# A two-layer trunk (gMLP mixer, retention, two dense MLPs): residual by tokens throughout, and four more blocks of products by seven

## The chip, the cores and the metric

The kernel runs on one core of a Trainium2 chip. A core has a matrix engine (TensorE: PE, with its weight loads PEld) and four others: VectorE (DVE), ScalarE (ACT), GpSimd (POOL) and SyncE (SP), which here only starts DMA transfers. DMA transfers are started from queues of SP, ACT and POOL and are carried out by 16 DMA engines. Matrix products add up in PSUM, in eight banks of 128 partitions x 512 float32. The metric is the device time of one execution, in us.

## The reference, cut to what matters

512 tokens of 1024 features, float32, go through two layers. Layer 0 mixes tokens by a gated MLP in chunks of 128, layer 1 by retention with four heads; each is followed by a dense MLP with a squared ReLU.

```python
def squared_relu_mlp(h, w1, w2):
    a = jax.nn.relu(h @ w1)
    return (a * a) @ w2
...
    proj = xn @ w_in                       # 1024 -> q 1024, k 1024, v 2048, g 2048
    q, k, v, g = jnp.split(proj, ...)
    q, k = rotary(q, cos, sin), rotary(k, cos, sin)
    # per head: scores of q and k with decay, causal, times v
    o = rmsnorm(o, head_norm_g.reshape(H, dv)).reshape(B, S, H * dv)
    o = (o * jax.nn.silu(g.astype(f32))).astype(xn.dtype)
    return o @ w_out
...
    for i in range(DEPTH):
        h = rmsnorm(x, norm_mix_g[i])
        x = x + mixer_i(h)                 # gMLP (w_in 1024x4096, w_out 2048x1024) or retention
        h = rmsnorm(x, norm_ffn_g[i])
        x = x + squared_relu_mlp(h, mlp_w1[i], mlp_w2[i])   # 1024x4096, 4096x1024
    return rmsnorm(x, final_norm_g)
```

## The kernel before

**Products.** Every float32 operand is split into a high part hi and a low part lo (fp32r), and `mm3` computes a product by three matmuls: hi hi, hi lo, lo hi. A matmul has 128 partitions of weights and 512 columns. Weights stream through the chip in raw tiles of 1 MB (one DMA on SP's queue, L166), each of two pieces: ACT casts a piece to its high half (`wH`, L234), DVE subtracts it for the low half (`wL`, L241). A piece feeds 24 matmuls, or twelve where it is half of a product by seven.

**Order.** `step` appends a piece and the function that uses it to a list, which is then run through: the function emits the matmuls, then `refill` the cast of the third piece ahead and the low half of the second ahead (LOOK = 3), then come its hooks (`behind`), and its evacuation. Each engine works through its own instructions in the order in which they were emitted. So what is emitted first on DVE also runs first, whoever waits.

**Products by seven.** `seven` computes a block of four 512x512 products of weights with activations by seven products (Strassen's scheme as changed by Winograd), numbered s = 0 to 6 in the order of a plan. Weight sums are made by accumulating DMAs on POOL's queue (`add_up`, L207): first the sum `t1`, then two more sums in the same tile once its pieces have been split, and one separate sum; so four accumulating DMAs for each `seven`. Activation sums are made by `form(s)`, on DVE and ACT: two sums (`sa`), two casts, two low parts (`sp`). Products gather in banks `a`, `b`, `c` (two PSUM tiles each: `smva0`, `smva1`), and DVE adds a finished one to its output (L529).

**Tiles and layers.** The residual `xT` stands by features (features on partitions). Its norm is summed over squares (ACT, POOL) and spread over partitions by matmuls with ones (`wide_stats`, `spread`); up products are evacuated by DVE with ReLU and the norm's factor (L953), then squared by ACT (L954). In layer 0's dense MLP three of four blocks are made by seven into `tok`, and the fourth by plain products (`dn`, `down_last`), where `tok` is transposed back on PE (L1023) and added to `xT`. After retention `to_tokens` (L1282) transposes `xT` the other way. In retention the values of heads 0 and 1 are made by seven, those of heads 2 and 3 plainly (`v_unit`), and all gates plainly by features (`g_unit`). q and k are rotated by DVE's four products with two tables, and POOL's two additions (L1084, L1085). `av` multiplies scores and values by features, with 512, 384, 256 and 128 columns, and the head's norm is again a sum over partitions.

**PSUM.** Six banks go by the name `acc`, two by `mis` (transposes, sums over partitions, scores, av).

## Time and profile before

| What | us |
|---|---|
| time, median of 3 runs | 1354.7 (1354.36 to 1355.17) |
| span of the profiled execution | 1353.1 |
| PE busy | 1342.5 |
| DVE busy | 868.0 |
| ACT busy | 581.0 |
| POOL busy | 190.3 |

The page gives for the profiled execution its span, from the first instruction to the last; the runs' times contain that and what lies around it, 1.6 us by the median. In a row of busy times, x is the number of instructions; in a row of a group the last numbers are the mean of one, or the least, median and greatest duration in ns. In the chain of waits and in the timeline a row begins with the start and the duration in us; a record of a matmul reaches into the next one. A raw tile is named with the array that it was loaded from, and the numbers of buffers are left out.

### The profile page before, as it was taken

What the parts mean: (1) busy time and instruction counts of PE and PEld (TensorE: products, weight loads), DVE (VectorE), ACT (ScalarE), POOL (GpSimd) and SP (SyncE); (2) the same over time, 40 slices, a digit from 0 to 9 for tenths busy, and PEclk for the clock granted to TensorE, in tenths of its full rate; (3) what the DMA queues carried; (4) which work ended last, traced back from release to release, by engine and by line L of the source; (5) the groups of instructions that cost most, each with busy time, mean ns of one, the idle gap of its engine ahead of it and who ended that gap; (6) DMA issues with size and microseconds to landing.
All of it is one profiled execution on the core that took longest, in us unless ns stands there. A gap on an engine that the chain in (4) does not pass through costs nothing.

```text
span 1353.1 us, 15298 instructions
## 1 busy us (share of the span) xinstructions
PE 1342.5 (99%) x6106; PEld 1117.2 (83%) x6106; DVE 868.0 (64%) x1101; ACT 581.0 (43%) x827; POOL 190.3 (14%) x145
## 2 busy tenths in 40 slices
PE   9999999999999999999999999999999999999997
PEld 7888888888888888888888888888888888888886
DVE  7754456665656656678946456557494675665697
ACT  5655443235544434524533343224333543443464
POOL 4100121130100000012201101111221000100003
PEclk9999999999999999999999999999999999999999
DMA  8662221245674747515712122221126375686763
GB/s 304 169 166 81 90 94 63 93 151 152 149 203 127 215 129 182 167 61 191 172 63 93 63 90 91 85 93 64 63 94 201 106 182 140 169 202 172 198 171 94
DMA packets 124439, 182.43 MB, mean 135 GB/s; under 512 B 3200, under 2 KB 68304, under 8 KB 124368
## 3 DMA queue, kind: packets, MB, share of 16 engines
q1 hardware_dynamic: 105040, 143.17, 31.2%
q0 software_dynamic: 19008, 37.75, 16.2%
q8 instruction: 48, 0.79, 0.2%
q10 hardware_dynamic: 320, 0.53, 0.1%
q14 instruction: 23, 0.19, 0.0%
HBM read 179.35 MB, written 2.10 MB: 134 GB/s over the span
## 4 chain that ended last, share of the span: by engine, by line
PE 97%; DVE 2%; ACT 1%; POOL 0%; issue 0%; ACTq 0%; POOLq 0%; DVEq 0%
PE up L281 24%; PE qk L281 6%; PE u L281 6%; PE o L281 6%; PE g L281 6%; PE ro L281 6%; PE dn L281 2%; PE vv L281 2%; PE av L281 2%; PE v L852 2%; PE smva L281 2%; PE smwa L281 2%; PE v L281 2%; PE sm12a L281 2%; PE sm11a L281 2%; PE sm10a L281 2%
## 5 line engine op out<-in xcount | busy, mean ns | idle before, releaser
L241 DVE TENSOR_TENSOR wL<-raw,wH 128x1024 fp32r<-128x1024 f32 x235 | 305.0, 1301 | 43.8 <-ACT wH L234 15.6
L234 ACT CAST wH<-raw 128x1024 fp32r<-128x1024 f32 x235 | 245.3, 1045 | 63.5 <-ACT wH L234 8.9
L281 PE MATMUL up<-hH,wH 128*128 128x512 f32 x480 | 187.2, 390 | 0.2 <-ACT xtok L1283 0.2
L281 PE MATMUL up<-hH,wL 128*128 128x512 f32 x480 | 186.8, 389 | 0.0
L281 PE MATMUL up<-hL,wH 128*128 128x512 f32 x480 | 186.8, 389 | 0.0
L953 DVE SCALAR_TENSOR_TENSOR r<-up,wide 128x512 f32<-128x512 f32 x54 | 37.4, 692 | 153.6 <-PE up L281 146.2
L954 ACT ACTIVATE aF<-r 128x512 f32<-128x512 f32 x54 | 34.2, 633 | 222.6 <-DVE r L953 222.6
L281 PEld LDWEIGHTS up<-hH,wH 128*128 128x128 f32 x480 | 90.1, 188 | 18.9 <-ACT xtok L1283 0.5
L281 PEld LDWEIGHTS up<-hH,wL 128*128 128x128 f32 x480 | 90.1, 188 | 18.9
L281 PEld LDWEIGHTS up<-hL,wH 128*128 128x128 f32 x480 | 90.1, 188 | 18.7
L207 POOL DMA_DIRECT2D raw<-in_mlp_w_dram x25 | 33.1, 1381 | 437.9 <-DVE wL L241 193.1
L310 POOL TENSOR_TENSOR ssq<-ssq,sq 128x512 f32<-128x512 f32 x28 | 44.1, 1577 | 117.0 <-ACT sq L309 116.7
L241 DVE TENSOR_TENSOR wL<-more,wH 128x1024 fp32r<-128x1024 f32 x42 | 51.0, 1217 | 4.5 <-issue 3.0
L234 ACT CAST wH<-more 128x1024 fp32r<-128x1024 f32 x42 | 44.0, 1047 | 15.9 <-ACT wH L234 6.0
L281 PE MATMUL o<-yH,wH 128*128 128x512 f32 x128 | 50.8, 396 | 0.0
L281 PE MATMUL g<-hH,wH 128*128 128x512 f32 x128 | 50.5, 394 | 0.0
L281 PE MATMUL u<-hH,wH 128*128 128x512 f32 x128 | 50.2, 393 | 0.0
L281 PE MATMUL qk<-hH,wH 128*128 128x512 f32 x128 | 50.0, 391 | 0.0
L281 PE MATMUL ro<-ryH,wH 128*128 128x512 f32 x128 | 49.9, 390 | 0.0
L281 PE MATMUL u<-hH,wL 128*128 128x512 f32 x128 | 49.9, 390 | 0.0
L281 PE MATMUL ro<-ryH,wL 128*128 128x512 f32 x128 | 49.9, 390 | 0.0
L281 PE MATMUL g<-hH,wL 128*128 128x512 f32 x128 | 49.9, 390 | 0.0
(450 smaller groups left out, 3050.1 us busy)
## 6 DMA issues: line engine op xcount, KB each, us to landing
raw<-in_mlp_w_dram SPq DMA_DIRECT2D x50, 1024.0 KB, 5.1
raw<-in_mlp_w_dram POOLq DMA_DIRECT2D x25, 1024.0 KB, 8.8
raw<-in_b_w_in_dram SPq DMA_DIRECT2D x22, 1024.0 KB, 5.0
more<-in_mlp_w_dram SPq DMA_DIRECT2D x21, 1024.0 KB, 5.3
raw<-in_a_w_in_dram SPq DMA_DIRECT2D x10, 1024.0 KB, 5.3
raw<-in_a_w_out_dram SPq DMA_DIRECT2D x8, 1024.0 KB, 4.9
raw<-in_b_w_out_dram SPq DMA_DIRECT2D x8, 1024.0 KB, 4.8
morew<-in_a_w_in_dram SPq DMA_DIRECT2D x5, 1024.0 KB, 8.5
```

What stands on the lines that cost most here:

```text
L207: nc.gpsimd.dma_start(out=r.tile, in_=src, accum_op=ALU.add)
L234: nc.scalar.copy(out=p.hi, in_=p.src)
L241: nc.vector.tensor_sub(out=p.lo, in0=p.src, in1=f32(p.hi))
L281: nc.tensor.matmul(ps, lhsT=a, rhs=b, start=start and i == 0, stop=stop and i == 2, skip_group_check=resumed)
L310: nc.gpsimd.tensor_tensor(out=state["ssq"], in0=state["ssq"], in1=sq, op=ALU.add)
L852: nc.tensor.matmul(accs0[n], lhsT=h[kk][:, n * P : (n + 1) * P], rhs=w, start=kk == 0 and j == 0, stop=kk == 7 and j == 2)
L953: nc.vector.scalar_tensor_tensor(out=r, in0=ps, scalar=0.0, in1=rbc, op0=ALU.max, op1=ALU.mult)
L954: nc.scalar.activation(a, r, AF.Square)
```

## The change

- **Residual by tokens.** `tok`, two tiles with tokens on partitions, holds the residual from x to the end. Inputs of products (`hH`, `hL`) are its transposes: `turn` on PE, then ACT (high part, with the norm's gain) and DVE (low part). The row's norm is a sum that ACT gathers along a row (`tsq`), and its factor is applied later: to q and k through the two tables, to values and gates as a row's scale, in the dense MLP as the squared factor `r2s` when a product is added to `tok` (a ReLU commutes with a positive factor). Up products are evacuated by ACT alone: ReLU and Square. x is loaded again in layer 0's mixer, since its tiles are used in between. Sums of the input (`hF`) are made by adding the parts.
- **Dense.** Layer 0's fourth block is made by seven as layer 1's is (`dense_end`); `down_last`, `to_tokens` and the sums over partitions are gone.
- **Retention.** All values and all gates are made by seven: `v` and `w` (values of heads 0, 1 and 2, 3), `g` and `j` (gates). The four sums of the input that V forms are stored in DRAM (`keep_sums`, SP's queue) and fetched for W and J (`fetched`, POOL's queue). `av` has tokens on partitions, and its result, multiplied by the gate and the head's norm, is transposed (`turned`). The rotation's additions are DVE's, and its tables lie in `wide`, where the norm's factors were broadcast.
- **Order.** A script, played by `play`, lists retention's pieces (q also for k, o and s for the output) with the work behind each in brackets.

```diff
-    xT2 = [big([P, 4, T], F32, f"xT{b}") for b in range(2)]
-    xT = [xT2[k // 4][:, k % 4, :] for k in range(KD)]
-    hH, hL = [None] * KD, [None] * KD
+    tok = [big([P, NT, 512], F32, f"tok{c}") for c in range(2)]
...
+    def turn(ps, k, ns=range(NT)):
+        for n in ns:
+            nc.tensor.transpose(ps[:, n * P : (n + 1) * P], tok[k // 4][:, n, (k % 4) * P : (k % 4 + 1) * P], ident)
+
+    def chunk(k, ps, gcol):
+
+        fresh_h(k, gcol)
         g = gT[:, gcol + k : gcol + k + 1]
-        nc.vector.tensor_scalar_mul(hH[k], xT[k], g)
-        nc.vector.scalar_tensor_tensor(out=hL[k], in0=xT[k], scalar=g, in1=f32(hH[k]), op0=ALU.mult, op1=ALU.subtract)
-
-    def squares(k, gcol):
-        if k == 0:
-            state["ssq"] = tmp(f"ssq{gcol}", "ssq", 1)
-            nc.scalar.activation(state["ssq"], xT[k], AF.Square)
-        else:
-            sq = tmp(f"sq{gcol}_{k}", "sq")
-            nc.scalar.activation(sq, xT[k], AF.Square)
-            nc.gpsimd.tensor_tensor(out=state["ssq"], in0=state["ssq"], in1=sq, op=ALU.add)
+        nc.scalar.activation(hH[k], ps, AF.Copy, scale=g)
+        nc.vector.scalar_tensor_tensor(out=hL[k], in0=ps, scalar=g, in1=f32(hH[k]), op0=ALU.mult, op1=ALU.subtract)
+
+    def turned_chunk(k, gcol, bank=mis):
+        ps = bank(f"ht{k}")
+        turn(ps, k)
+        chunk(k, ps, gcol)
+
+    def add_parts(b):
+        whole[b] = big([P, 4, T], F32, f"hF{4 * b}")
+        for i in range(4):
+            nc.vector.tensor_add(out=whole[b][:, i, :], in0=f32(hH[4 * b + i]), in1=f32(hL[4 * b + i]))
+
+    def tsq(n, c):
+        nc.scalar.activation(tmp(f"tsq{n}{c}", "sq"), tok[c][:, n, :], AF.Square, accum_out=ssf[:, n, c : c + 1])
...
+    def root(dst, power):
+
+        a = work.tile([P, NT], F32, tag="ms", name="ms", bufs=2)
+        nc.vector.tensor_tensor(out=a, in0=ssf[:, :, 0], in1=ssf[:, :, 1], op=ALU.add)
+        nc.vector.tensor_scalar(out=a, in0=a, scalar1=1.0 / D, scalar2=EPS, op0=ALU.mult, op1=ALU.add)
+        nc.gpsimd.tensor_tensor(out=dst, in0=a, in1=power[:, 0:NT], op=ALU.pow)
...
+    def norm(name):
+
+        root(r4, mhalf)
+        yield
+        yield from spread(r4, rbc, name)
+
+    def norm_squares():
+
+        root(r2s[:, 0, :], mone)
+        nc.vector.tensor_scalar(out=r2s[:, 1, :], in0=r2s[:, 0, :], scalar1=-1.0, scalar2=0.0, op0=ALU.mult, op1=ALU.add)
...
+        def add_to(m, n, t, op, bank):
+
+            m, n = 2 * m + t, 1 - n if swap else n
+            v, sign = dst[n][:, m, :], op == ALU.subtract
+            if (m // 2, n) in fresh:
+                nc.scalar.activation(v, bank, AF.Copy, scale=-1.0 if sign else 1.0)
+            elif scaled:
+                nc.vector.scalar_tensor_tensor(out=v, in0=bank, scalar=r2s[:, int(sign), m : m + 1], in1=v, op0=ALU.mult, op1=ALU.add)
+            else:
+                nc.vector.tensor_tensor(out=v, in0=v, in1=bank, op=op)
...
+    def out_half(pl, ys, c, name, hooks={}, after=None, end=None):
+
+        accs, last = {}, 2 * len(pl) - 1
+
+        def mms(p, i, n):
+            for k in range(2):
+                kk = 2 * i + k
+                mm3(accs[n], *ys(kk, n), p.hi[:, k, :], p.lo[:, k, :], kk == 0, kk == last)
+
+        def add(n):
+            v = tok[c][:, n, :]
+            nc.vector.tensor_tensor(out=v, in0=v, in1=accs[n], op=ALU.add)
...
-            if ("rbc", l) in state:
-                r = zt(f"r{i}")
-                nc.vector.scalar_tensor_tensor(out=r, in0=ps, scalar=0.0, in1=rbc, op0=ALU.max, op1=ALU.mult)
-                nc.scalar.activation(a, r, AF.Square)
-                return
             nc.scalar.activation(a, ps, AF.Relu)
-            while ("rbc", l) not in state:
-                yield
-            nc.vector.tensor_mul(a, a, rbc)
             nc.scalar.activation(a, a, AF.Square)
-            yield
+            return iter(())
...
-    def down_last(gcol, ahead):
-
-        pl = pieces_f(mlp_w2[0], (3072, 4096), (0, D))
-        ev = evac_x(gcol)
-
-        def back(i):
-            ps = mis(f"yt{i}")
-            for n in range(NT):
-                nc.tensor.transpose(ps[:, n * P : (n + 1) * P], tok[i // 4][:, n, (i % 4) * P : (i % 4 + 1) * P], ident)
-            nc.vector.tensor_add(xT[i], xT[i], ps)
...
+    def dense_end(l, plan3, ahead, hooked, after3, last, more, middle=None):
+
+        pl = pieces_f(mlp_w1[l], (0, D), (3072, 4096))
+        hooks2, hooks3 = {}, {}
+        _, form2, prod2 = seven(mlp_w2[l], 2048, 0, side_a(4, f"{l}2"), tok, f"{l}2", (0, 1, 2, 3, 5, 4, 6), hooks2, scaled=True)
+        t3, form3, prod3 = seven(mlp_w2[l], 3072, 0, side_a(6, f"{l}3"), tok, f"{l}3", plan3, hooks3, after3, last, True, True, middle=middle)
...
+    def keep_sums(s):
+
+        stored[s] = dram.tile([P, 2, 4, T // 2], F32, name=f"sums{s}")
+        nc.sync.dma_start(out=stored[s], in_=f32(made["v", s]))
+
+    def fetched(s):
+        if s in (0, 2, 6):
+            return direct_h(s)
+        sp = big([P, 2, 4, T // 2], F32R, f"spx{s}")
+        nc.gpsimd.dma_start(out=sp, in_=stored[s])
+        return side_split(sp)
+
+    def twofold(c, dst, side, name, plan, swap=False):
+        return seven(bw, 0, c, side, dst, name, plan, swap=swap, new=True, auto=False)
+
+    PLAN_V = (0, 2, 1, 3, 4, 5, 6)
+    PLAN_G = (1, 4, 0, 3, 5, 2, 6)
+    sides = [kept(side_h("v")), kept(fetched)]
+    tV, form_v, prodV = zip(*[twofold(VW + 1024 * i, vF[i], sides[i], "vw"[i], (PLAN_V, PLAN_G)[i]) for i in range(2)])
+    tG, form_g, prodG = zip(*[twofold(GWT + 1024 * i, gF[i], sides[i], "gj"[i], PLAN_G, True) for i in range(2)])
...
-        nc.gpsimd.tensor_tensor(out=m[0], in0=m[0], in1=m[1], op=ALU.subtract)
-        nc.gpsimd.tensor_tensor(out=m[2], in0=m[2], in1=m[3], op=ALU.add)
+        nc.vector.tensor_sub(out=m[0], in0=m[0], in1=m[1])
+        nc.vector.tensor_add(out=m[2], in0=m[2], in1=m[3])
...
+    def av(h, n):
+
         vhi, vlo = vv[h]
         ph, pl = pp[h]
-        ps = mis(f"av{h}{c}")
-        cs = slice(c * P, (c + 1) * P)
-        for j in range(NT):
-            s = slice(POFF[j], POFF[j] + T - j * P)
-            mm3(ps[:, j * P :], vhi[:, j, cs], vlo[:, j, cs], ph[:, s], pl[:, s], j == 0, j == NT - 1)
+        assert {(x, h, j) for x in "pv" for j in range(n + 1)} | {("g", h, n)} <= ready, (h, n)
+        ps = mis(f"av{h}{n}")
+        for j in range(n + 1):
+            s = slice(POFF[j] + (n - j) * P, POFF[j] + (n - j + 1) * P)
+            mm3(ps, ph[:, s], pl[:, s], vhi[:, j, :], vlo[:, j, :], j == 0, j == n)
 
         def gen():
-            o = oo[h][:, c, :]
-            if c == 0:
-                state["ssqh"] = tmp(f"ssqh{h}", "ssq", 1)
-                nc.scalar.activation(state["ssqh"], ps, AF.Square)
+            y, ss, ms, r = gates(h)[:, n, :], ssh[:, h, n : n + 1], msh[:, h, n : n + 1], rh[:, h, n : n + 1]
+            nc.vector.tensor_tensor(out=y, in0=ps, in1=y, op=ALU.mult)
+            nc.scalar.activation(tmp(f"sqh{h}{n}", "sq"), ps, AF.Square, accum_out=ss)
+            yield
+            nc.vector.tensor_scalar(out=ms, in0=ss, scalar1=1.0 / DV, scalar2=EPS, op0=ALU.mult, op1=ALU.add)
+            rsqrt(r, ms, 1)
+            nc.scalar.activation(y, y, AF.Copy, scale=r)
+            ready.add(("y", h, n))
...
+        for n in range(NT):
+            nc.tensor.transpose(ps[:, n * P : (n + 1) * P], gates(h)[:, n, c * P : (c + 1) * P], ident)
+        g = gT[:, HG + 4 * h + c : HG + 4 * h + c + 1]
+        hi, lo = rH[h][:, c, :], rL[h][:, c, :]
+        nc.scalar.activation(hi, ps, AF.Copy, scale=g)
+        nc.vector.scalar_tensor_tensor(out=lo, in0=ps, scalar=g, in1=f32(hi), op0=ALU.mult, op1=ALU.subtract)
...
+    play("""
+        Q(w1,w0,R) v v v v(f1,k1) v(R,N) v(f3) q q v(f4) v v(f5,k4) v v(k5) v v(k3) v +G g g g(sc00,sc01)
+        g(sc02,sc03,vs00) g(vs01) g q g(vs02,vs03) g q g g g(si001) g(si02) q(si03,av03) q(av00,av02) g
+        q(sc10,sc11,si10) g(av01,sc12) q(si12,si13,sc13,vs10123) q(yt00,si11,yt01) q(yt02,av101,F3) o(yt03,av123)
+        o(yt10123) o(F4) +w o w o o w(F5) w o o w w w w w(F1) w w +j j w j w w(sc20) j w j(sc21,sc22) j(vs20) j(sc23)
+        q(vs22,vs23) j j(vs21) j q j(si21,si20,av21) q(si23,si22,av22,av20) q(av23) j(sc30,sc32) j(sc31)
+        j(yt20123,vs3012) -(vs33,si301) j(sc33) s(si323,av30123) s(yt30123) s s s(sq0123,ht0) s(ht2,ht3) s(ht1)
+    """, v=prodV[0], g=prodG[0], w=prodV[1], j=prodG[1], o=out_pair(0), s=out_pair(1, half_end(FFN + 8)),
+        Q=qs[:1], q=qs[1:])
```

On DVE before the change, where values of heads 0 and 1 are made by seven, from the third sum's operations (`sav`, `spv3`) on; `vF` is the output of values, `m01` the rotation of k of head 0 (L1080 to L1083):

```order
L618 SCALAR_TENSOR_TENSOR sav_4573<-xT0_86,gT_76,sav_4573 128x256 x4
L646 SCALAR_TENSOR_TENSOR spv3_4796<-sav_4573,spv3_4796 128x512 x2
L241 TENSOR_TENSOR wL146_4791<-raw67_4105,wH146_4790 128x1024
L529 TENSOR_TENSOR vF0_4545<-vF0_4545,smvb0_4772 128x512
L529 TENSOR_TENSOR vF0_4545<-vF0_4545,smvb1_4773 128x512
L241 TENSOR_TENSOR wL147_4818<-raw67_4105,wH147_4817 128x1024
L1080 TENSOR_TENSOR m010_4853<-qk02_4741,tab_4547 128x512
L1081 TENSOR_TENSOR m013_4856<-qk02_4741,tab_4547 128x512
L1082 TENSOR_TENSOR m011_4854<-qk03_4823,tab_4547 128x512
L1083 TENSOR_TENSOR m012_4855<-qk03_4823,tab_4547 128x512
L241 TENSOR_TENSOR wL148_4849<-raw74_4684,wH148_4848 128x1024
L618 SCALAR_TENSOR_TENSOR sav_4573<-xT1_87,gT_76,sav_4573 128x256 x4
```

Between two low halves stands one form, one pair of additions or one rotation's products. After the change, the same place starts with the first form, behind piece 147:

```order
L249 TENSOR_TENSOR wL149_4615<-raw71_4249,wH149_4614 128x1024
L593 TENSOR_TENSOR sav_4638<-hF0_4552,hF4_4547 128x512 x2
L616 TENSOR_TENSOR spv1_4637<-sav_4638,spv1_4637 128x512 x2
L503 TENSOR_TENSOR vF00_4597<-vF00_4597,smvb0_4600 128x512
L503 TENSOR_TENSOR vF00_4597<-vF00_4597,smvb1_4601 128x512
L249 TENSOR_TENSOR wL150_4631<-raw75_4545,wH150_4630 128x1024
L350 TENSOR_TENSOR sp_mix1_1_4668<-r4_80,sp_mix1_0_4667 128x4
L365 TENSOR_TENSOR dg0_mix1_4671<-ident_74,sp_mix1_0_4667 128x512
L365 TENSOR_TENSOR dg1_mix1_4673<-ident_74,sp_mix1_1_4668 128x512
L1243 TENSOR_TENSOR wide_79<-trg1_4466,wide_79 128x512
L1244 TENSOR_TENSOR wide_79<-trg0_4465,wide_79 128x512
L1138 TENSOR_TENSOR m000_4695<-qk0a_4473,wide_79 128x512
```

The additions of `smvb` stand behind the form; then come the norm's diagonals (`dg`, for the broadcast `wide`), the two tables (into `wide`) and the rotation of q, all before low half 151. The rotation's other two products and its two additions, low half 151 and the low parts of q (`qkL`), form 3, low halves 152 and 153, and a second rotation with its additions follow, then these:

```order
L249 TENSOR_TENSOR wL154_4781<-raw77_4635,wH154_4780 128x1024
L599 TENSOR_TENSOR sav_4638<-sav_4638,hF4_4547 128x512 x2
L616 TENSOR_TENSOR spv4_4818<-sav_4638,spv4_4818 128x512 x2
L249 TENSOR_TENSOR wL155_4815<-raw77_4635,wH155_4814 128x1024
L249 TENSOR_TENSOR wL156_4838<-raw78_4709,wH156_4837 128x1024
L602 TENSOR_TENSOR sav_4638<-hF0_4552 128x512 x2
L616 TENSOR_TENSOR spv5_4861<-sav_4638,spv5_4861 128x512 x2
L249 TENSOR_TENSOR wL157_4858<-raw78_4709,wH157_4857 128x1024
L503 TENSOR_TENSOR vF01_4723<-vF01_4723,smvc0_4649 128x512
L503 TENSOR_TENSOR vF01_4723<-vF01_4723,smvc1_4650 128x512
L249 TENSOR_TENSOR wL158_4883<-raw71_4249,wH158_4882 128x1024
L249 TENSOR_TENSOR wL159_4903<-raw71_4249,wH159_4902 128x1024
```

Forms 4 and 5 come, with one low half or two between, ahead of the additions of `smvc`, which come ahead of low halves 158 and 159.

On POOL before, the sums for values by seven (`raw67`, three times in one tile) stood between the rotation's additions:

```order
L207 DMA raw67_4105<-in_b_w_in_dram 128x4x512
L1084 TENSOR_TENSOR m000_4725<-m000_4725,m001_4726 128x512
L1085 TENSOR_TENSOR m002_4727<-m002_4727,m003_4728 128x512
L207 DMA morev0_4543<-in_b_w_in_dram 128x4x512
L207 DMA raw67_4105<-in_b_w_in_dram 128x4x512
L1084 TENSOR_TENSOR m010_4853<-m010_4853,m011_4854 128x512
L1085 TENSOR_TENSOR m012_4855<-m012_4855,m013_4856 128x512
```

After the change POOL holds sums for V (`raw71`, `raw78`), G (`raw80`, `raw85`) and W (`raw93`), the head norm's powers (`rh`) and the fetches (`spx`):

```order
L215 DMA raw71_4249<-in_b_w_in_dram 128x4x512
L215 DMA raw78_4709<-in_b_w_in_dram 128x4x512
L215 DMA raw71_4249<-in_b_w_in_dram 128x4x512
L215 DMA raw80_4785<-in_b_w_in_dram 128x4x512 x2
L215 DMA raw85_5058<-in_b_w_in_dram 128x4x512
L215 DMA raw80_4785<-in_b_w_in_dram 128x4x512
L336 TENSOR_TENSOR rh_90<-msh_89,mhalf_85 128x1 x4
L215 DMA raw93_5587<-in_b_w_in_dram 128x4x512
L336 TENSOR_TENSOR rh_90<-msh_89,mhalf_85 128x1 x2
L1069 DMA spx3_5752<-sums3_4942 128x2048
L336 TENSOR_TENSOR rh_90<-msh_89,mhalf_85 128x1 x2
L1069 DMA spx4_5916<-sums4_4868 128x2048
```

The rotation's additions are gone from this queue; G's first sum (`raw80`) stands behind two sums for V, and fetches stand between W's.

724 lines of the change are left out of this document (325 added, 399 removed).

## The prediction, as recorded before the result was known

> **What bounds the kernel now.** I read the shares of busy time first, then what TensorE waited for, then the clock by stages, and the chain of waits last, for the price of a matmul.
>
> ```profile
> span 1353.1 us, 15298 instructions
> PE 1342.5 (99%) x6106; PEld 1117.2 (83%) x6106; DVE 868.0 (64%) x1101; ACT 581.0 (43%) x827; POOL 190.3 (14%) x145
> PE 97%; DVE 2%; ACT 1%; POOL 0%; issue 0%; ACTq 0%; POOLq 0%; DVEq 0%
> ```
> ```profile
> PE warm L1395 <- POOL ident masks.py:199: 1.4, 1, 1.4
> PE av L281 <- DVE pL L1140: 0.3, 1, 0.3
> PE up L281 <- ACT xtok L1283: 0.2, 1, 0.2
> ```
> PE is busy for 99% of the span, 97% of the chain is its work, and the second list holds all its waits: 1.9 us. So the time is the sum of PE's instructions, every one of them removed is gained, and a wait of PE that the change brings is lost in full.
>
> The next view gives stretches: busy time of PE, weight load, DVE, ACT and POOL, granted clock, DMA share, GB/s.
>
> ```profile
> 110.00:250.00 140.00, 140.00 (x688) 118.30 (x686) 74.88 (x91) 61.13 (x92) 22.47 (x17) 1.00 0.24 79
> 620.00:696.00 76.00, 76.00 (x336) 62.76 (x336) 60.84 (x78) 39.80 (x56) 14.87 (x10) 1.00 0.58 158
> 1290.00:1300.00 10.00, 10.00 (x46) 8.28 (x45) 9.59 (x13) 6.90 (x9) 0.00 (x0) 1.00 0.54 186
> 1346.00:1353.10 7.10, 0.00 (x0) 0.00 (x0) 2.41 (x5) 2.06 (x4) 1.21 (x3) 0.69 0.39 148
> ```
> Layer 0's mixer (110 to 250) has much room. Where values are made by seven products (620 to 696) DVE is busy for 80%; at 1290, in the last layer's end, for 96%, and PE still waits for nothing. The tail without PE is 7.1 us.
>
> Prices of PE's work, from the chain (start, length, what):
>
> ```profile
> 343.48 5.44 PE sm00c L281 x24
> 348.92 5.44 PE up L281 x24
> 354.36 5.44 PE sm00b L281 x24
> ...
> 589.62 5.49 PE dn L281 x24
> 595.55 5.50 PE dn L281 x24
> ...
> 727.60 5.54 PE g L281 x24
> 735.00 5.50 PE g L281 x24
> 742.36 5.50 PE g L281 x24
> ```
> 24 matmuls of 512 columns end 5.44 us apart: **0.2267 us each** (a record's 390 ns overlaps the next). Between the two dn rows stand four transposes: 595.55 − 589.62 − 5.49 = **0.44 us**. Between two g rows stands one block of av, twelve matmuls (three each of 512, 384, 256, 128 columns): 742.36 − 735.00 − 5.50 = **1.86 us**.
>
> **The change, part by part.** *PE's sum*, by the counts of instructions:
> - Four blocks of products go from eight products to seven: layer 0's last dense block (−24 matmuls), the values of heads 2 and 3 (−24), both pairs of gates (−48): 96 × 0.2267 = −21.8.
> - av with tokens as rows has 120 matmuls of 512 columns in place of 16 blocks: 120 × 0.2267 = 27.2 against 16 × 1.86 = 29.8, −2.6.
> - Matmuls that sum squares across partitions and broadcast them: 26 become 4: −22 × 0.2267 = −5.0.
> - Transposes go from 96 to 192: 24 groups of four more, × 0.44 = +10.6.
>
> Together −21.8 − 2.6 − 5.0 + 10.6 = **−18.8**. No term of it is a guess except that the new transposes cost as much as those between the dn rows.
>
> *DVE where the values begin.* The prices, from the last layer's end, where DVE works without a pause (start, duration, what), then an evacuation's hand-over:
>
> ```profile
> 1295.79 1.28 DVE L529 TENSOR_TENSOR xtok<-xtok,sm12a 128x512 f32<-128x512 f32 x2
> 1296.99 1.22 DVE L241 TENSOR_TENSOR wL<-raw,wH 128x1024 fp32r<-128x1024 f32 x1
> 1298.12 1.29 DVE L596 TENSOR_TENSOR sp<-aF,sp 128x512 fp32r<-128x512 f32 x2
> ```
> ```profile
> 1295.83 1.05 ACT L234 CAST wH<-raw 128x1024 fp32r<-128x1024 f32 x1 [0.85 <-PE sm12a L281]
> 1296.78 1.14 ACT L593 CAST sp<-aF 128x512 fp32r<-128x512 f32 x2
> ```
> ```profile
> 343.09 0.39 PE L281 MATMUL up<-hH,wL 128*128 128x512 f32 x1
> 343.32 0.39 PE L281 MATMUL sm00c<-wH,sp 128*128 128x512 f32 x1
> 343.52 0.69 DVE L953 SCALAR_TENSOR_TENSOR r<-up,wide 128x512 f32<-128x512 f32 x1 [4.20 <-PE up L281]
> ```
> A 512-wide operation costs DVE 1.20/2 = 0.60, a low half of weights 1.13; ACT's cast of weights takes 0.95. DVE reads a bank 0.2 after the next matmul's slot begins.
>
> After the change DVE's rows from smvb's additions to the low parts of the fifth sum are seven low halves (150 to 156) and 34 operations of 512: two additions, three forms of four, two rotations of eight (two of them POOL's before), two diagonals, two tables. That is 7 × 1.13 + 34 × 0.60 = 28.3 us, while PE's pieces 148 to 155 (six halves of 2.72 and two q pieces of 5.44) give 27.2. DVE begins late, behind a form, and pauses where a rotation waits for q. Low halves run two pieces ahead of PE; additions and sums have no such lead. Walked by hand, with 0 where PE begins piece 147 and rows priced as above:
> - Low half 149 and the first form's four operations keep DVE until 3.85; then smvb's first addition ends at 4.5. Piece 148 wants that bank (of six, q's two are held until the rotation) and would start at 2.72: it starts at 4.6, **1.9**.
> - The broadcast waits for its second diagonal, **0.15**; q's third piece wants a bank that the rotation's first and fourth products free at 11.2 instead of 10.6: **0.7**.
> - The fourth and fifth sums' low parts come **1.35** and **0.55** late; the last product waits for the fifth's addition on the same bank, **0.85**.
>
> The sum is **+5.5**. Its bounds: 0, as where at 1290 a DVE at 96% never stopped PE; and 5.5 + 5.4 = 11, if low halves too are late by their whole lead. One row says that DVE can be slower still:
>
> ```profile
> L241 DVE TENSOR_TENSOR wL<-raw,wH x15: 1209/1219/2321, 622.0 to 693.7; 128x1024 fp32r<-128x1024 f32 x15
> ```
> The longest of these fifteen is 2.3 us, twice the median. With less on POOL this should be rarer.
>
> *DMA.* Queues (packets, MB, share of 16 engines) and single transfers (us to landing):
>
> ```profile
> q1 hardware_dynamic: 105040, 143.17, 31.2%
> q0 software_dynamic: 19008, 37.75, 16.2%
> ```
> ```profile
> raw<-in_mlp_w_dram POOLq DMA_DIRECT2D x25, 1024.0 KB, 8.8
> raw<-in_b_w_in_dram SPq DMA_DIRECT2D x22, 1024.0 KB, 5.0
> more<-in_mlp_w_dram POOLq DMA_DIRECT2D x3, 1024.0 KB, 8.6
> raw<-in_b_w_in_dram POOLq DMA_DIRECT2D x3, 1024.0 KB, 8.4
> morev<-in_b_w_in_dram POOLq DMA_DIRECT2D x1, 1024.0 KB, 8.3
> ```
> From the first: 143.17 / (0.312 × 1353.1) = 0.339 MB a us on SP's queue, 37.75 / (0.162 × 1353.1) = 0.172 on POOL's. Over V's seven products and q's pieces PE takes 54 us; seven raw loads, four stores of sums and a decay table (11.8 MB) need 34.8 us of all 16 engines, five accumulating loads (5.2 MB) 30.5: 65 in 54. Loads ahead of the stretch take some of it off. The gates' first sum, put behind two others on POOL's queue, lands, at 1.049/0.172 = 6.1 us a transfer one behind another, some 4 us before it is needed. Bounds 0 and 6; I take **+2**, nearer to 0, as the sums of the dense layers were never late.
>
> The Trainium skill (*DMA: Bandwidth & Descriptors*, "Anatomy of one DMA — SWDGE (gpsimd) path") fits 2.0 us plus bytes / 436e3 us, 4.4 us by estimate for such a transfer; the trace has 8.4 for one that accumulates, so the measurement decides. By the page this term would be 0 and the time 1342.4.
>
> *Small hand-overs* (three norms whose transposes follow additions directly, the turned y before the out product, fewer raw slots): each has a row of zero now; at most 0.43 (343.52 − 343.09) for some fifteen of them, 6.5; I take **+1**.
>
> *At nothing:* ReLU and Square go to ACT whole (64 more 512-wide, 64 × 0.6 = 38 us, spread over ACT's 57% idle time); x is fetched again where DMA stands at 0.24; 24 pieces of PE, over 80 us, lie between a sum's store and its first fetch; layer 0's last sum leads PE by 0.8 us; weights are prepared as before, 24 low halves more (24 × 1.13 = 27 us of DVE) against 68 fewer of its 512-wide operations (41 us). If the cover at layer 0's end is gone, it costs one form, 2.4.
>
> Net: −18.8 + 5.5 + 2 + 1 = **−10.3**. The profiled execution's span is 1353.1, the runs' median 1354.7, 1.6 more; I keep that: span 1342.8, **1344.4 us**.
>
> **The rivals.**
> - *Cover holds everywhere*: no new wait, 1354.7 − 18.8 = **1335.9**. For it: 1290 to 1300, and the lead of weights. Against: additions at the values' begin stand behind a form and have no lead.
> - *DMA is the bound* in values and gates: all 6 us of excess there in place of 2, and 2 more in W and J: 1344.4 + 4 + 2 = **1350**. For: 65 in 54. Against: loads of earlier stretches run ahead.
> - *The clock*: in the tail, where PE stands idle, 0.69 was granted. If a new wait took the clock down, the matmuls behind it would run slower; 7.1 us of matmuls at 0.69 take 3.2 longer; three such: 1344.4 + 9.6 = **1354**, no change. Against: the longest wait that I walk is 1.9 us, and no row of before shows a lower clock at a short wait. The Trainium skill (*TensorE: Matmul & The Clock Gate*, "What's actually happening") lets an idle window of about 3.4 us halve the clock; the 0.69 in an idle 7.1 us agrees with it, and none of my waits is that long.
> - *Slower: sums come late.* Retention gets sixteen accumulating loads (four before), eight of them onto a freshly loaded tile: 5.0 + 8.4 + 0.95 + 1.13 = 15.5 us from a free slot to a usable weight. The cover is two products, 10.9, once the lead is used up, and spare slots are gone here. Each late by 4.6: 8 × 4.6 = 37, 1354.7 − 18.8 + 37 = **1373**. It decides from (18.8 + 2.7) / 8 = 2.7 us for each of the eight. For: POOL's queue is serial and now also fetches the stored sums. Against: four such sums before, and 28 in the dense layers, stopped PE for nothing, and q, o pieces stand between products.
>
> **How the numbers follow.** Forecast 0.55; cover 0.20; DMA 0.12; clock 0.04; late sums 0.09. The forecast's own range is 1338 to 1350 (its waits from 2 to 14). The range of 8 in 10 goes from 1334 (cover, with transposes a little cheaper) to 1354; late sums lie outside, and the edges of the others. A run tells about 0.2% from no change, 2.7 us, so faster is below 1352.0: all of cover, nearly all of the forecast, three quarters of DMA, 0.55 × 0.96 + 0.20 + 0.09 = 0.82; slower above 1357.4: 0.09 and a little of the rest, 0.10; same 0.08.
>
> **What would show it.** PE's instructions: a span shorter by 18.8 less its waits, rows of 24 still 5.44 apart. DVE: a wait of PE before the first smvc, and smaller ones before smva and qk, at DVE's additions and spv. DMA: waits whose releaser is a cast or low half of raw tiles. Wrong would be: transposes at much over 0.44 a group; a wait at each sum; a granted clock under 1.00 in the values.

## The result, and the profile after

| What | before | after |
|---|---|---|
| time, median, us | 1354.57 (1354.36 to 1355.17) | 1342.93 (1342.79 to 1343.91) |
| span of the profiled execution, us | 1353.1 | 1341.3 |

The change makes the kernel 11.6 us faster: ratio 0.9915, 95% interval 0.9901 to 0.9929. The forecast was 1344.4.

First the page of the changed kernel (span, busy times), then all the waits of TensorE in it (what it waited for: us in total, times, longest):

```profile
span 1341.3 us, 15169 instructions
PE 1325.6 (99%) x6012; PEld 1099.9 (82%) x6012; DVE 798.5 (60%) x1005; ACT 656.5 (49%) x967; POOL 126.8 (9%) x113
```
```profile
PE smvc L289 <- DVE vF L503: 1.7, 1, 1.7
PE smvc L289 <- ACT spv L613: 1.5, 1, 1.5
PE warm L1391 <- POOL ident masks.py:199: 1.4, 1, 1.4
PE qk L289 <- DVE m L1139: 0.7, 1, 0.7
PE smja L289 <- DVE gF L503: 0.6, 1, 0.6
PE yt L1223 <- ACT gF L1210: 0.2, 1, 0.2
```

PE's busy time falls by 16.9 us, and 5.1 of the gain in work goes into idle time: the span falls by 11.8. The first, second and fourth row are where the values begin, as the walk had them (1.9, 1.35, 0.7). No row names a DMA, nor a cast or low half of weights, by which the prediction would have known it.

Where the time came from is seen in the chain of waits at four places that both kernels have: the first up piece of layer 0, the begin of retention, the first up piece of layer 1, the end. Before (start, length, what):

```profile
282.87 4.76 PE up00a L281 x21
...
619.29 5.49 PE smva L281 x24
...
1013.37 4.76 PE up10a L281 x21
```
After:

```profile
285.18 2.77 PE up00a L289 x12
...
615.25 2.74 PE qk0a L289 x12
...
1005.04 2.77 PE up10a L289 x12
```

| Stretch | before | after | difference |
|---|---|---|---|
| start and layer 0's mixer | 282.87 | 285.18 | +2.3 |
| layer 0's dense MLP | 336.42 | 330.07 | −6.3 |
| retention | 394.08 | 389.79 | −4.3 |
| layer 1's dense MLP, end | 339.7 | 336.3 | −3.5 |

Retention saves 72 of the 96 matmuls, 16.3 us at 0.2267, and yields only 4.3. There lie the new transposes of y, and all the waits and slow matmuls told below.

Two losses have no row among the waits: the low clock, and the slow restart behind a wait. In these two stretches (busy time of PE, weight load, DVE, ACT, POOL; granted clock, DMA share, GB/s) the wait of 1.5 us stands in the first, and the clock is at 0.72 in the second:

```profile
660.00:664.00 4.00, 2.77 (x13) 1.96 (x11) 3.58 (x5) 1.85 (x3) 0.00 (x0) 1.00 1.12 204
664.00:670.00 6.00, 5.72 (x17) 4.25 (x18) 5.06 (x7) 4.55 (x8) 0.00 (x0) 0.72 1.14 210
670.00:690.00 20.00, 20.00 (x90) 16.58 (x89) 13.11 (x14) 10.60 (x13) 1.28 (x1) 1.00 1.06 336
```

In half-microsecond steps the clock is 0.50 from 665.7 to 669.1. The chain through this place shows both the wait's making and its price:

```profile
639.22 3.01 PE smvc L289 x12
...
646.15 11.19 PE qk L289 x48
...
657.37 0.69 DVE m L1140
658.06 0.60 DVE m L1141
658.66 0.61 DVE m L1142
...
659.29 0.63 ACT qkH L1147
...
659.94 1.29 DVE qkL L1148 x2
661.24 1.14 DVE wL L249
662.37 1.22 DVE sav L599 x2
...
663.61 0.63 ACT spv L613
...
664.28 7.62 PE smvc L289 x24
```

q's last piece ends, the second rotation starts on DVE and goes on to its low parts, then come a low half and the fourth form; the product that needs it starts at 664.28. Its 24 matmuls take 7.62 us instead of 5.44. How much of that is the clock's is seen in the run without stores (below), where the same product starts after the same wait of 1.51 and no low clock follows: from its first matmul to the next product's it takes 5.85 us there, 7.45 here. So the clock has **1.6**, and the restart 0.6: a record of a matmul reaches 0.16 past its slot, and the first three intervals behind the wait are 0.34, 0.39 and 0.34 instead of 0.23. The two other waits have a restart of 0.3 each (3.01 for twelve matmuls instead of 2.72, 11.19 for 48 instead of 10.88).

Over the whole stretch the low clock costs less than 1.6. In the run without stores, PE waits 0.6 us for an addition of DVE's ahead of the last product of V, by its list of waits:

```profile
PE smva L289 <- DVE vF L503: 0.6, 1, 0.6
```

Here the slow product hides that wait. From the fourth product's start to the gates' first product it is 18.50 us here and 17.78 there, 0.7 more.

The ledger, in the prediction's terms: PE's work −18.8, waits where the values begin 1.71 + 0.69 + 1.51 = +3.9, the restarts behind them +1.2, the clock +1.6, hand-overs 0.6 + 0.2 = +0.8, two waits of before gone −0.5. That is −11.8, as much as the spans differ by; that it comes out to a tenth is chance, since the restarts of the smaller waits are not in it.

### The profile page after: what moved, and what is told of

It reads as the page before. It is cut to its first block, busy times and chain, and to the rows that moved or that the text cites. A ratio compares the mean times of both kernels' runs of the same rounds, so it can differ in the third digit from the quotient of the medians.

```text
span 1341.3 us, 15169 instructions
## 1 busy us (share of the span) xinstructions
PE 1325.6 (99%) x6012; PEld 1099.9 (82%) x6012; DVE 798.5 (60%) x1005; ACT 656.5 (49%) x967; POOL 126.8 (9%) x113
## 4 chain that ended last, share of the span: by engine, by line
PE 94%; DVE 2%; ACT 2%; POOL 1%; issue 1%; ACTq 0%; POOLq 0%; DVEq 0%
PE up L289 24%; PE o L289 7%; PE u L289 6%; PE ro L289 6%; PE qk L289 5%; PE smwa L289 3%; PE v L875 2%; PE smga L289 2%; PE v L289 2%; PE sm01a L289 2%; PE smwc L289 2%; PE sm12a L289 2%; PE sm00a L289 2%; PE sm11a L289 2%; PE sm10a L289 2%; PE sm02a L289 2%
## 5 line engine op out<-in xcount | busy, mean ns | idle before, releaser
L242 ACT CAST wH<-raw 128x1024 fp32r<-128x1024 f32 x265 | 276.4, 1046 | 169.0 <-DMA raw<-in_b_w_in_dram 32.6
L976 ACT ACTIVATE aF<-up 128x512 f32<-128x512 f32 x60 | 36.0, 600 | 219.1 <-PE up L289 219.1
L289 PEld LDWEIGHTS up<-hH,wH 128*128 128x128 f32 x480 | 90.1, 188 | 18.8
L616 DVE TENSOR_TENSOR sp<-aF,sp 128x512 fp32r<-128x512 f32 x48 | 31.0, 688 | 52.1 <-ACT sp L613 52.1
L289 PE MATMUL o<-wH,yH 128*128 128x512 f32 x128 | 51.0, 399 | 0.0
L289 PE MATMUL ro<-wH,ryH 128*128 128x512 f32 x128 | 50.7, 396 | 0.0
L289 PE MATMUL ro<-wH,ryL 128*128 128x512 f32 x128 | 50.1, 392 | 0.1
L289 PE MATMUL o<-wH,yL 128*128 128x512 f32 x128 | 50.0, 390 | 0.0
L289 PE MATMUL ro<-wL,ryH 128*128 128x512 f32 x128 | 49.9, 390 | 0.0
L289 PE MATMUL o<-wL,yH 128*128 128x512 f32 x128 | 49.9, 390 | 0.0
L289 PE MATMUL u<-hL,wH 128*128 128x512 f32 x128 | 49.9, 390 | 0.0
## 6 DMA issues: line engine op xcount, KB each, us to landing
raw<-in_b_w_in_dram POOLq DMA_DIRECT2D x16, 1024.0 KB, 10.7
```

The source lines that it names most:

```text
L242: nc.scalar.copy(out=p.hi, in_=p.src)
L289: nc.tensor.matmul(ps, lhsT=a, rhs=b, start=start and i == 0, stop=stop and i == 2, skip_group_check=resumed)
L616: nc.vector.tensor_sub(out=lo, in0=vs[c], in1=f32(hi))
L976: nc.scalar.activation(a, ps, AF.Relu)
```

## The experiments

Times are given against the changed kernel's 1342.9 (span 1341.3); ratios are to the kernel before, measured with it on one chip.

### Additions on POOL, and a q piece ahead

The first theory (A): DVE has too much work where the values begin. Rivals: the banks alone (B'), DMA (B), and POOL beside DVE (C). Edit of the first run, then of the second; the third has both.

```diff
-        nc.vector.tensor_sub(out=m[0], in0=m[0], in1=m[1])
-        nc.vector.tensor_add(out=m[2], in0=m[2], in1=m[3])
+        (nc.gpsimd if h == 0 else nc.vector).tensor_tensor(out=m[0], in0=m[0], in1=m[1], op=ALU.subtract)
+        (nc.gpsimd if h == 0 else nc.vector).tensor_tensor(out=m[2], in0=m[2], in1=m[3], op=ALU.add)
```
```diff
-                out.append(lambda hook, p=pl[i], evac=evac, n=2 * which + i: feat(p, hs, evac, f"qk{h}{n}", hook, acc, h > 0))
+                out.append(lambda hook, p=pl[i], evac=evac, n=2 * which + i: feat(p, hs, evac, f"qk{h}{n}", hook, mis if h == 0 else acc, h > 0))
...
-        Q(w1,w0,R) v v v v(f1,k1) v(R,N) v(f3) q q v(f4) v v(f5,k4) v v(k5) v v(k3) v +G g g g(sc00,sc01)
+        Q(w1,w0,R) v v v v(f1,k1) q v(R,N) v(f3) q v(f4) v v(f5,k4) v v(k5) v v(k3) v +G g g g(sc00,sc01)
```

> The two additions of head 0's rotations go back to POOL; all else as in the changed kernel. In the changed kernel's profile TensorE waits 1.71 us before the first smvc piece, 0.69 before q, 1.51 before the fourth product (for the cast of its sum), and right after the last of these the granted clock is 0.50 for some 3 us, which costs 2.0 us more. Theory A (DVE has too much work in this stretch): DVE loses four operations of 0.60, 2.4 us; the wait of 1.51 goes, the clock stays at 1.00, the other two waits stay: 3.5 us less, span about 1337.8. Theory B (DMA is the bound here, its share being over 1.00 from 652 on): the wait moves to a cast that waits for a raw tile, gain under 1 us. Theory C (DVE is slowed by POOL on operations beside it): some of DVE's low halves take 2.3 us and the gain is lost.

Measured: 1346.9, ratio 0.9941 (0.9927 to 0.9956), span 1345.3: 4 us **slower** than the changed kernel. The wait for the fourth product's sum is 4.0 instead of 1.5, and the clock stays low for twice as long. Why is on POOL's timeline (start, length, what, idle before and its end) and in a row of DVE:

```profile
657.59 2.60 POOL L215 DMA_DIRECT2D raw<-in_b_w_in_dram  x2 [1.07 <-DMA raw<-in_b_w_in_dram]
659.11 2.39 POOL L1142 TENSOR_TENSOR m<-m,m 128x512 f32<-128x512 f32 x1
660.37 2.38 POOL L1143 TENSOR_TENSOR m<-m,m 128x512 f32<-128x512 f32 x1
```
```profile
649.81 2.29 DVE L1148 TENSOR_TENSOR qkL<-m,qkH 128x512 fp32r<-128x512 f32 x2 [0.24 <-ACT qkH L1147]
```

The two additions together take 3.6 us (their records overlap), where DVE has 0.6 for each. They end at 662.8, on DVE they ended at 659.9. That they stand behind two accumulating loads on POOL's queue, which wait for a raw tile, costs them little: the first starts 0.2 us after DVE has made what it reads (658.9). The rest of the delay comes from before: beside the first rotation's additions on POOL, two low parts on DVE take 2.29 instead of 1.29 (the row above), and the second rotation starts 0.8 us later than in the changed kernel, counted from the first wait of the values. Theory C held; A's gain was not seen, and that DVE has the additions is a gain of the change.

> Order alone: the third of head 0's q and k pieces goes ahead of the first smvc piece, and these two pieces take banks of the other pool (mis). Theory A (DVE's work sets the pace): the waits of 1.71 and 0.69 go, but the third and fourth forms are no earlier, so smva waits for the third form by about 1 us and the fourth product begins no earlier than before; with the clock's loss the span is within 1 us of 1341.3. Theory B' (the waits come from the banks alone): 2.4 us less, 1338.9.

Measured: 1355.6, ratio 1.0007 (0.9997 to 1.0016), span 1354.4, the whole gain lost. Neither theory had this. The waits of 1.7 and 0.7 are gone, as said; one of 10.1 has come, that of 1.5 has grown to 4.2, and the clock is at 0.50 for 20.5 us in and behind the two. The long wait, the end of ACT's wait that made it, and the load's issue on POOL:

```profile
PE bc_mix L369 <- DVE dg_mix L365: 10.1, 1, 10.1
```
```profile
653.48 1.04 ACT L242 CAST wH<-raw 128x1024 fp32r<-128x1024 f32 x1 [15.07 <-DMA raw<-in_b_w_in_dram]
```
```profile
641.04 1.32 POOL L215 DMA_DIRECT2D raw<-in_b_w_in_dram  x1 [8.96 <-issue]
```

This is the second sum in one tile (`t2` over `t1`): it can be issued only when `t1`'s last low half is made. In the changed kernel the two q pieces stand behind that, and ACT's wait is short (its row, and the issue):

```profile
646.92 1.06 ACT L242 CAST wH<-raw 128x1024 fp32r<-128x1024 f32 x1 [3.60 <-DMA raw<-in_b_w_in_dram]
```
```profile
636.19 1.32 POOL L215 DMA_DIRECT2D raw<-in_b_w_in_dram  x1 [3.80 <-DVE wL L249]
```

From the issue to the cast it is 10.7 us there and 12.4 here. With a q piece moved ahead of `t1`'s product the sum is issued 4.9 us later, and the casts, emitted in order, hold back what ACT does next: the norm's cast, without which neither the diagonals nor the broadcast can be made. This is the prediction's rival "sums come late", brought about by one piece of 5.44 us moved.

> Both edits: additions of head 0's rotations on POOL, and the q piece ahead. Theory A: DVE's 2.4 us are saved and no bank is waited for; the fourth product begins some 2.3 us earlier than in the changed kernel, with a wait near 1 us ahead of the third or fourth product; where that does not bring the clock down, 4.3 us less (1337.0), where it does, 2.3 (1339.0). Theory B (DMA): gain under 1 us, with waits for raw tiles at the gates' first sums.

Measured: 1359.1, ratio 1.0032 (1.0019 to 1.0045): slower than the kernel before. Both losses are there: a wait of 9.9 for the diagonals and one of 6.7 for the fourth sum.

### DMA: the stores twice, and none

```diff
+        again = dram.tile([P, 2, 4, T // 2], F32, name=f"again{s}")
+        nc.sync.dma_start(out=again, in_=f32(made["v", s]))
```

> The four stores of V's sums are made twice (a second copy that nobody reads): 4.2 MB more on SP's queue in the values, 12.4 us of all DMA engines by the rate of before's profile (0.339 MB a us). My step on DMA said that values and gates have 65 us of transfers in 54 us of TensorE's work and priced that at 2 us. If DMA is at its limit there, the gates' first sums land some 10 us later, their margin of 3.4 us is gone, and the time grows by 5 to 9 us. If there is room, nothing changes (under 1 us).

Measured: 1351.3, ratio 0.9976 (0.9967 to 0.9985), 8.4 slower, within the range for "at its limit". But not by the gates' first sums: two q pieces wait for weights, that is, for a plain load that SP's queue issued at 687.87, ten us after the stores, and that took 16.9 us to land. The DMA share stayed over 1.00 until 705; in the changed kernel it is at 0.82 from 690 on and 0.33 from 695 on. Behind these waits the clock is at 0.50 for 6.8 us more.

```profile
PE qk L289 <- DVE wL L249: 3.1, 1, 3.1
PE smvc L289 <- ACT spv L613: 2.2, 1, 2.2
PE qk L289 <- ACT wH L242: 1.8, 1, 1.8
```

The other side, which leaves out the stores and fetches part of a weight matrix in place of the sums (the output is not the reference's):

```diff
-        stored[s] = dram.tile([P, 2, 4, T // 2], F32, name=f"sums{s}")
-        nc.sync.dma_start(out=stored[s], in_=f32(made["v", s]))
+        stored[s] = mlp_w2[0, 0:256, :].rearrange("(p a) n -> p (a n)", p=P).rearrange("p (j k t) -> p j k t", j=2, k=4)
```

> The four stores of V's sums are left out, and W and J fetch other data of the same size (the output is not the reference's): 4.2 MB less to write in the stretch where the DMA share is over 1.00. This prices the step that I put at 2 us, with the doubled stores (8.4 us slower) as the other side. If DMA is full but still hidden in the changed kernel: within 0.7 us of it. If it already delays TensorE there: 2 us or more faster.

Measured: 1342.5 (1342.0 to 1343.0), ratio 0.9911 (0.9896 to 0.9925): not to be told from the changed kernel, and the waits of 1.7, 1.5 and 0.7 are the same. In the 60 us concerned the DMA share falls from 0.91 (first fence, the changed kernel) to 0.76 (second):

```profile
640.00:700.00 60.00, 57.79 (x252) 47.06 (x251) 45.08 (x62) 28.60 (x41) 5.19 (x4) 0.97 0.91 252
```
```profile
640.00:700.00 60.00, 57.20 (x256) 46.33 (x255) 45.52 (x63) 29.55 (x42) 5.19 (x4) 1.00 0.76 184
```

So DMA is nearly full there, costs the changed kernel nothing that can be measured, and has no room for four stores more.

### Undoing one block of seven

```diff
-    dense_end(0, (1, 0, 2, 3, 5, 6, 4), {5: "30", 6: "24", 7: "35", (5, 0): "31", (6, 0): "32", "10": "33", "00": "34", "30": "36"}, {}, {
...
+        for reg in out_half(pieces_y(mlp_w2[0], (3072, 4096), 0), acts, 0, "dn", scaled=True):
+            reg()
+        for reg in out_half(pieces_y(mlp_w2[0], (3072, 4096), 1), acts, 1, "dn", {
+            0: lambda: ([tsq(n, 0) for n in range(NT)], turned_chunk(0, LATE), turned_chunk(1, LATE)),
+            1: lambda: (turned_chunk(2, LATE), turned_chunk(3, LATE))}, end=half_end(LATE), scaled=True):
+            reg()
```

> Layer 0's fourth dense block is undone: plain products with tokens as rows in two halves, as layer 0's mixer ends, in place of seven products. TensorE gets 24 matmuls of 512 more, 24 x 0.2267 = 5.4 us. By the prediction's first term (an eighth of the products, all of it on TensorE's path): 5.4 us slower than the changed kernel, span 1346.7. If the sums of that block cost as much as they save: no difference.

Measured: 1348.2, ratio 0.9954 (0.9939 to 0.9968): 5.2 us slower, span 1346.4 against 1346.7 expected. From layer 0's first up piece to the begin of retention it takes 335.6 us, the changed kernel 330.1: 5.5 us more, where 24 matmuls make 5.4. So the block's saving lies on PE's path in full, and its sums cost nothing. What differs after that has another cause: no low clock follows the wait of 1.5 in this run, PE waits 0.6 ahead of the last product of V as in the run without stores, and 1.3 instead of 0.6 for the gates' additions (`smja`).

### DVE's order, and half of the sums on ACT

```diff
-        Q(w1,w0,R) v v v v(f1,k1) v(R,N) v(f3) q q v(f4) v v(f5,k4) v v(k5) v v(k3) v +G g g g(sc00,sc01)
+        Q(w1,w0,R) v v v(R) v(f1,k1) v(N) v(f3) q q(f4) v v v(f5,k4) v v(k5) v v(k3) v +G g g g(sc00,sc01)
```

> Order alone, without moving a piece of TensorE: the norm's diagonals are made one piece earlier, and the fourth form stands behind the second q piece, ahead of the second rotation, in place of behind the third product. Theory A (DVE's order in this stretch, not DMA, sets the four waits of the changed kernel): the fourth product's sum is ready in time, the wait of 1.51 and the half clock after it (2.07) go, the first wait grows by 0.4, the one before q shrinks by 0.4: about 3.5 us less than the changed kernel, span 1337.8. Theory B (DMA): the time stays within 1 us of the changed kernel, since the next raw sum is awaited instead.

Measured: 1344.8, ratio 0.9929 (0.9913 to 0.9946), span 1342.7: not faster, at the edge slower; theory A's 3.5 us did not come. The fourth sum is in time, and PE waits 2.3 us for the low half of the same product's weights, which now stands behind the rotation; the clock is low behind this wait too.

```profile
PE smvc L289 <- DVE wL L249: 2.3, 1, 2.3
```
```profile
656.61 1.29 DVE L599 TENSOR_TENSOR sav<-sav,hF 128x512 f32<-128x512 f32 x2
...
663.56 1.29 DVE L1148 TENSOR_TENSOR qkL<-m,qkH 128x512 fp32r<-128x512 f32 x2
664.77 3.49 DVE L249 TENSOR_TENSOR wL<-raw,wH 128x1024 fp32r<-128x1024 f32 x3
```

The work ahead of the product is the same, in whatever order. That sharpens theory A: it is the second rotation that doesn't fit between q's end and the fourth product (A').

```diff
+        if gcol == MIX + 8 and k // 4 in (1,):
+            if k % 4 == 0:
+                whole[1] = big([P, 4, T], F32, "hF4")
+            nc.scalar.activation(whole[1][:, k % 4, :], ps, AF.Copy, scale=g)
...
-        Q(w1,w0,R) v v v v(f1,k1) v(R,N) v(f3) q q v(f4) v v(f5,k4) v v(k5) v v(k3) v +G g g g(sc00,sc01)
+        Q(w0,R) v v(f1,k1) v(R) v v(N) v(f3) q q(f4) v v v(f5,k4) v v(k5) v v(k3) v +G g g g(sc00,sc01)
```

> As e5, and half of the input's sums (hF4, four operations) is made by ACT from the transposes, so that the first form can stand two pieces earlier and the diagonals behind it. Theory A: DVE reaches smvb's additions when TensorE has finished them, and all four losses go (1.71, 0.69, 1.51 and 2.07, together 6.0): span about 1335.5 to 1336.5. Theory B (DMA): the gates' first sum, cast in the changed kernel at 676.8 with 3.4 us to spare, is now awaited for 2 to 3 us: span 1338 to 1339.

Measured: 1345.9, ratio 0.9933 (0.9918 to 0.9948), span 1344.0. The first wait is gone. But ACT makes each part of hF4 between two evacuations of transposes, and PE now waits for those:

```profile
PE smvc L289 <- DVE wL L249: 3.0, 1, 3.0
...
PE qk0a L289 <- ACT hH L318: 1.1, 2, 0.6
```

### The second rotation moved, and all together

```diff
+        for _ in range(13 if (h, which) == (0, 1) else 0):
+            yield
```

> One thing is moved: the second rotation (q's tables on k of head 0, six operations on DVE and two low parts), from between the third and the fourth product of V to behind the last, beside the gates' first product; TensorE's order stays. Theory A' (formed after the fifth experiment: DVE is given 3.6 us of rotation and 2.4 of low parts and casts between the end of q's last piece and the fourth product, which leaves 5.4 us, so either the sum or the low half is late whatever their order): the wait of 1.5 before the fourth product goes and with it the low clock where it followed; the waits of 1.7 and 0.7 stay: span 1337.7 to 1339.3. Theory B (DMA): the gates' first sum is awaited instead: span 1340 or more.

Measured: 1345.9, ratio 0.9934 (0.9921 to 0.9946), span 1343.9: 3 us slower than the changed kernel, where A' had 1337.7 to 1339.3 for the span and B 1340 or more. The wait of 1.5 and the low clock are gone, as A' said. But the rotation at its new place stands ahead of the low halves of the gates' first weights, whose raw sum has come late (its last packets end at 680.2, in the changed kernel at 676.4), and PE waits there:

```profile
PE smgc L289 <- DVE wL L249: 2.5, 2, 1.7
...
PE smgc L289 <- ACT wH L242: 0.9, 1, 0.9
```

The next run has the rotation there too, with hF4 on ACT behind the evacuations, the first form two pieces earlier, and the broadcast a piece ahead of the tables:

```diff
+        if gcol == MIX + 8:
+            whole[1] = big([P, 4, T], F32, "hF4")
+            for k in range(4, KD):
+                nc.scalar.activation(whole[1][:, k % 4, :], late[k], AF.Copy, scale=gT[:, gcol + k : gcol + k + 1])
...
+        for _ in range(13 if (h, which) == (0, 1) else 0):
+            yield
...
-        Q(w1,w0,R) v v v v(f1,k1) v(R,N) v(f3) q q v(f4) v v(f5,k4) v v(k5) v v(k3) v +G g g g(sc00,sc01)
+        Q(w0,R) v v(f1,k1) v(R) v(R) v(N) v(f3) q q v(f4) v v(f5,k4) v v(k5) v v(k3) v +G g g g(sc00,sc01)
```

> As e9, and ahead of it: hF4 by ACT behind the transposes' own evacuations, the first form two pieces earlier, the norm's diagonals at the third product and its broadcast one piece ahead of the tables. Theory A': the waits of 1.7 and 0.7 go too: span 1335.5 to 1336.5. Theory B (DMA): the raw sum for the gates lands as late as before while TensorE is 6 us earlier: a wait of 2 to 3 us for it, span 1338 to 1339.

Measured: 1340.0 (1339.1 to 1340.9), ratio 0.9892 (0.9877 to 0.9907), span 1337.3, between the two theories. All three waits of the values and the low clock are gone, and the gates' first product starts 6.4 us earlier (676.0 instead of 682.6, of which 0.3 is an earlier start of layer 0's up pieces). Of that 2.1 came back at the gates; the raw sum is what ACT waits for there:

```profile
PE smgc L289 <- DVE wL L249: 2.1, 2, 1.7
PE warm L1397 <- POOL ident masks.py:199: 1.4, 1, 1.4
PE smja L289 <- DVE gF L503: 0.8, 1, 0.8
```
```profile
674.40 2.00 ACT L242 CAST wH<-raw 128x1024 fp32r<-128x1024 f32 x2 [6.52 <-DMA raw<-in_b_w_in_dram]
```

In the changed kernel this cast began at 676.8, so the sum comes 2.1 us earlier by the same count, while PE is 6.4 us earlier. Both theories hold a part.

The last run of this kind differs from that one by the place of the rotation, two steps earlier:

```diff
-        for _ in range(13 if (h, which) == (0, 1) else 0):
+        for _ in range(11 if (h, which) == (0, 1) else 0):
```

> As e10, with the second rotation one place earlier: into the 4.4 us in which DVE waits for the cast of the gates' first sum, ahead of the low half 160 in place of behind it. In e10 TensorE waits 1.69 for the low half 161 behind the rotation and 0.42 for 160, whose raw sum comes late. If the rotation's place is the cause of the first, 1.7 us less than e10 (span 1335.6, time about 1338.3); the 0.4 by DMA stays. If the low half 161 is late for the raw sum itself, no gain.

Measured: 1339.2 (1338.6 to 1340.8), ratio 0.9891 (0.9875 to 0.9908), span 1336.9: 0.4 less by the span, where 1.7 were expected. The wait of 1.7 behind the rotation is gone, as expected. But the raw sum's cast begins at 675.77, 1.2 later than in the run before by the same count, so that the waits at the gates are still 1.3 instead of 2.1:

```profile
PE smgc L289 <- DVE wL L249: 0.8, 1, 0.8
...
PE smgc L289 <- ACT wH L242: 0.5, 1, 0.5
```

The last two can't be told apart by time. Both beat the changed kernel: every run of theirs (1338.6 to 1340.9) is below every run of it (1342.8 to 1343.9), though they were not run on one chip with it and the intervals of the ratios to the kernel before touch.

### What brings the clock down

```diff
+    def stall(n):
+        pa = mis("pa")
+        nc.tensor.transpose(pa[:, 0:P], ident, ident)
+        t = tmp("stall", "sq")
+        nc.scalar.copy(out=t[:, 0:P], in_=pa[:, 0:P])
+        for _ in range(n):
+            nc.scalar.copy(out=t, in_=wide[:, 0:T])
+        pb = mis("pb")
+        nc.tensor.transpose(pb[:, 0:P], t[:, 0:P], ident)
+        nc.scalar.copy(out=t[:, 0:P], in_=pb[:, 0:P])
...
+                    if l == 0:
+                        do(lambda n=(1, 2, 3, 4, 5, 6, 2, 3)[i - 1] if q == 0 else (4, 3, 2, 5, 3, 2, 4, 1)[i - 1]: stall(n))
```

> Not a version: sixteen waits of chosen length (about 1 to 4 us) are put into layer 0's dense part, each by a chain of one to six ACT copies between two small transposes, behind an up piece and a whole product or two away from the next. It asks which wait brings the clock down. If length alone decides, all waits over some length are followed by a granted clock of 0.50, and none under it. If the clock goes by fixed stretches of some 3.4 us, as the length of the low stretches in the runs so far suggests (3.4, 7, 14 us), waits of 1.5 to 3 us are followed by a low clock in some places and not in others, and only those of over about 3.4 always.

Measured (one run, 1427.2 us), from the waits in the timeline and the clock in steps of 0.1 us:

```
wait, us    places    followed by 0.50 in    length of the low stretch, us
2.04        2         1                      3.41
2.69        4         1                      6.83
3.34        4         4                      3.41, once 6.83
3.99        3         3                      3.41
4.64        2         2                      3.41
5.29        1         1                      6.83
```

A wait of 2.69 is followed by a low clock in one place of four, one of 2.04 in one of two: length alone does not decide. The twelve low stretches begin on one grid: their starts are whole multiples of 3.413 us apart, to 0.01. So the clock is set in fixed stretches, and a wait counts by how it lies in them: the four that had no effect were split over two stretches, with at most 1.82 us in either.

The kept traces of all runs, each with its own grid, bear that out, but without a sharp limit. Each of the 20 stretches at full clock in which PE stood idle for 1.98 us or more was followed by a low one. Of 29 with 1.0 to 1.82 us of idle time only two were: the one with 1.51 in the changed kernel, and one with 1.3, made up of short waits, in the run with half of the sums on ACT. In that run a wait of 2.98, split into 1.44 and 1.54, had no effect. In the runs with the plain fourth block and without stores the wait of 1.5 was split. But a wait of 1.51 that lay whole in one stretch had no effect in retention of the run with sixteen waits, nor had waits of 1.69 to 1.71 in four other runs. What decides under 2 us stays open.

## Why the prediction was right, point by point

**PE's sum, −18.8: right.** Busy time fell by 16.9 although 1.6 of slow matmuls and 1.2 of restarts were added; by busy time the work fell by 19.7, by the ledger of the spans by 18.8. The new transposes cost what those of before did; the run that undoes one block took 5.5 more up to retention, where the sum has 5.4.

**DVE where the values begin, +5.5: mechanism right, size 3.9.** Three waits came where they were walked to (1.9, 0.7, 1.35 against 1.71, 0.69, 1.51). What PE waited for last was the fourth sum's high part from ACT, where the walk had its low parts. The smaller ones (0.15, 0.55, 0.85) did not show, but one of them was hidden by the slow product: without the low clock PE waits 0.6 for an addition ahead of the last product of V, where the walk had 0.85. The restarts behind the three waits (1.2) the walk left out. That the amount of DVE's work is the bound was shown by moving it about: a new order inside the stretch only moved the wait, and it went when the second rotation and half of the input's sums left DVE's share of the stretch, with the first form earlier too.

**DMA, +2: wrong by its size, nothing.** 65 us of transfers in 54 was the right reading only for the end of the stretch: from 618 to 672 the DMA share is 0.80, from 658 to 690 it is over 1.00. An accumulating load takes longer than before (second fence of the prediction's DMA part: 8.4), and four stores more cost 8.4 us. But a transfer that is late isn't yet a wait of PE. Taking the stores out gained nothing that can be measured. The row for the loads of retention now:

```profile
raw<-in_b_w_in_dram POOLq DMA_DIRECT2D x16, 1024.0 KB, 10.7
```

**Hand-overs, +1: right**, 0.8.

**The clock, not in the sum: wrong.** I kept it as a rival on the ground that no wait I walked was long enough. One of 1.51 was, once, and cost 1.6 in the product behind it and 0.7 over the stretch, where the rival put 3.2 for one. The Trainium skill (*TensorE: Matmul & The Clock Gate*, "What's actually happening") has about 3.4 us as the window; the 3.41 here agrees. That a shorter wait inside one window can be enough, the sentence as I used it does not say; the measurement decides.

**The rival "slower, sums come late"** stayed away from the changed kernel, but is as near as one piece: the run with q ahead and the changed kernel differ by 5.44 us of cover for one chained sum, and by 12.7 us of time. I had priced the eight sums onto fresh tiles; the one that struck was a chained one.

That the time came within 1.5 us of the forecast owes something to chance: 1.6 for the clock and 1.2 for restarts were not foreseen, while 2 for DMA and 1.6 of DVE's waits were foreseen and did not come.

## What to carry to other kernels

Where one engine is the bound, count its instructions first: the sum held to 1 us, and nearly everything else was a matter of single waits at one place and of what follows a wait. Before a piece of work is moved to close a wait, ask which transfer it has been covering: moving one q piece opened 10.1 us where 2.4 were to be gained. A wait that goes from one operand to another when the order changes (sum, low half, raw sum) belongs to the amount of work between two fixed points, and goes only if work leaves that stretch.
